# Two edits to the order of work: a weight split ahead of candidate steps, and a yield in the last attention

## The chip, the cores and the metric

The kernel runs on one core of a Trainium2 chip. The metric is the device time of one execution in microseconds, the median of several runs; shorter is better. A core has five engines with an instruction queue each: TensorE (PE in the profile) for matmuls, VectorE (DVE), ScalarE (ACT), GpSimd (POOL) and SyncE (SP), which issues most of the DMAs. Each queue is worked off in order; semaphores hold an instruction until its inputs are there.

## What is computed

One transformer layer on 1024 tokens of width 1024, batch 1, with float32 inputs. The parts that matter here:

```python
proj = h @ w_in[l]                       # q, k, v of 8 + 8 heads, forget logits
fox_out = forgetting_attention(...)      # causal softmax with a log-forget bias
sb_out = stick_breaking_attention(...)   # causal, in log space, a cumulative sum per row
x = x + gt1 * (mixed @ w_out[l])
h2 = rms_norm(x, g_norm_ffn[l]) * (1.0 + sc2) + sh2
x = x + gt2 * peer_layer(h2, w_query[l], sub_keys[l], expert_down[l], expert_up[l])
return rms_norm(x, g_final)

def peer_layer(h, w_query, sub_keys, expert_down, expert_up):
    query = (ht @ w_query).reshape(t, PEER_HEADS, 2, PEER_HALF)
    sub_scores = jnp.einsum('thpd,hpkd->thpk', query, sub_keys)
    half_vals, half_idx = lax.top_k(sub_scores, PEER_TOPK)           # 16 of 128, twice
    cand = half_vals[:, :, 0, :, None] + half_vals[:, :, 1, None, :]
    top_vals, top_pos = lax.top_k(cand.reshape(...), PEER_TOPK)      # 16 of the 16 x 16 sums
    ...                                                              # expert numbers, softmax gates
    act = gelu(jnp.einsum('td,thkd->thk', xb, expert_down[eb])) * gb
    return jnp.einsum('thk,thkd->td', act, expert_up[eb])
```

## The kernel before

The 1024 tokens are eight tiles of 128. Tiles 0 to 4 form block A, tiles 5 to 7 block B. Each block goes through norm, projection (`proj`), `attention`, output projection (`post`), second norm (`post_b`) and routing (`route`). Routing takes the 16 half-heads one after another: a panel of 24 matmuls with weights split into a high and a low part, the key scores, and the top 16 of 128 by VectorE's MAX, FIND_INDEX and MATCH_REPLACE (L886 to L890). From eight (head, tile) rows at a time `cands` (L930) forms the 50 candidate sums that can be among the top 16 (L946 to L951), searches them (L958 to L962), unpacks the positions (L966 to L978), picks the expert numbers bit by bit (L982 to L999) and makes the gates (L1004 to L1018). It is a generator: each `yield` ends a step. Up to L978 there are seven steps. Block A's candidates run inside its routing; block B's three generators are kept (`b.rest`, L924) for later.

In the front, streams of such generators are merged by `mrg` (L276): each stream has a weight and a count of credit that its yields have cost so far, and the stream with the least credit per weight is taken next. `mrg((rA, TOT_RB), (attention(bB, mixB, atp), TOT_B))` at L1149 merges the rest of block A's routing (weight 60) with block B's attention (weight 70). What the streams issue is then put into the engines' queues by a scheduler that has its own estimate of times, so that the order in a queue is not the order of the calls.

The feed-forward layer is done in two ways. For tiles 5 to 7 (`sparse`, L1208) the rows of the 128 experts of a token are gathered from HBM by GpSimd (L1221, L1234) and worked on by VectorE (L1223, L1239). For tiles 0 to 4 all 16384 experts are computed densely in 128 chunks of 128 experts; block A's gates lie in HBM as a dense table. A chunk's weights `wfd` and `wfu` are loaded by SP (L1270, L1272), split into high and low parts (`dh`, `uh` on ScalarE, L1289 and L1297; `dl`, `ul` on VectorE, L1292 and L1300), multiplied (`gelu_s`, L1302, two halves of 24 matmuls into the PSUM tile `sp`, GELU on ScalarE at L1308), multiplied by the gates (`mul_g`, L1310) and split again. After four chunks `up` (L1328) multiplies with the second weights. In this stage the order on TensorE, VectorE and ScalarE is that of the calls among themselves; instructions of the front may stand between them. Between the dense calls, `sp_(n)` issues n steps of block B's remaining candidates and then of the gathers: `sp_(PUMP_0)` with 7 steps at L1369, two steps in the first chunk, one and one in the later ones, five and two in the second half of a group.

Of the kernel before, what the change touches and what calls it, by code (L numbers as in the profile page):

```python
# [50 lines left out]
PUMP_0 = 7  # L51
# [54 lines left out]
def tile_kernel(ctx: ExitStack, tc: tile.TileContext, x, ccol, w_ada, badac, bgt2, gcols, w_in, w_f, bf_, gout,  # L106
# [473 lines left out]
    def attention(b, mixed, pool):  # L580
# [4 lines left out]
        def load_kq(pi):  # L585
            t = [pool.tile([P, b.ht], F32R, name=n_, tag=n_) for n_ in ("qa", "qb")]
            for n_, t_ in enumerate(t):
                dma(t_.bitcast(F32), qsp[pi, n_, :, qs_].bitcast(F32))
            t.append(pool.tile([P, b.ht], F32R, name="qla", tag="qla"))
            for h_ in (la, lb):  # L590
                dma(t[2][h_].bitcast(F32), qsp[pi, 2, la, qs_].bitcast(F32))
            k = [pool.tile([P, nk_], F32R, name=n_, tag=n_) for n_ in ("ka", "kb")]
            for n_, t_ in enumerate(k):
                dma(t_.bitcast(F32), ksp[pi, n_, :, 0:nk_].bitcast(F32))
            fb = pool.tile([P, nk_], F32, name="fb", tag="fb")
            dma(fb, fcd[pi:pi + 1, 0:nk_].to_broadcast([P, nk_]))
            L[pi] = t + k + [fb]
# [3 lines left out]
        def load_v(pi):  # L601
            vv = pool.tile([P, nk_], F32, name="vv", tag="vv")
            dma(vv, vsp[pi, :, 0:nk_])
            LV[pi] = vv
            LB[pi] = pool.tile([P, b.ht], F32R, name="qlb", tag="qlb", bufs=b.nq)
            for h_ in (la, lb):
                dma(LB[pi][h_].bitcast(F32), qsp[pi, 2, lb, qs_].bitcast(F32))
# [5 lines left out]
            yield -1  # L613
        load_kq(0)
        load_v(0)
        n = 8 * nt
        U = {}
        pair = {}
# [505 lines left out]
    atp = pool(st_at, "atA", 2)  # L1124
    mixA = xtile(xp, bA, "mixA")
    mrg((attention(bA, mixA, atp), 110), (ad2, max(1.0, 24 - AD1)), bg=((pp, PP2), (zr, ZR2)))
    st_at.close()
    rp = rpl[0] = pool(rps, "rp", side="right")
# [18 lines left out]
    mixB = xtile(xp, bB, "mixB")  # L1147
    soft_rs[0] = RS1
    mrg((rA, TOT_RB), (attention(bB, mixB, atp), TOT_B))  # L1149
    st_at.close()  # L1150
    am[0], ax[0] = ALS[2]()
# [94 lines left out]
    def pump(n):  # L1246
        while n > 0 and bgs:
            if next(bgs[0], 0) == 0:
                bgs.pop(0)
            else:  # L1250
                n -= 1
# [23 lines left out]
    def loadg(gi):  # L1275
        i1 = gi * CG
        dma = nc.sync.dma_start if gi > 1 else G.dma_start
        gg = dp.tile([P, CG, P], F32, name="gg", tag="gg", bufs=2)
        g2 = dp.tile([P, CG, P], F32, name="gg2", tag="gg2", bufs=1)
        for k in range(2):  # L1280
            dma((gg, g2)[k], gds[k].rearrange("(p c t) o -> p c (t o)", p=P, t=P)[:, i1:i1 + CG])
        g4 = dp.tile([P, NPT * P // SB, CG, SB], F32, name="g4", tag="g4", bufs=2)
        dma(g4, gd[:, :, i1 * SB:(i1 + CG) * SB].rearrange("s p (c t) -> p s c t", t=SB))
        return gg, g4, g2

    def split_d(k, act):
        if act:
            k.dh = dp3.tile([P, D], F32R, name="dh", tag="dh", bufs=2)
            S.activation(k.dh, k.wfd, AF.Copy)  # L1289
        else:  # L1290
            k.dl = dp3.tile([P, D], F32R, name="dl", tag="dl", bufs=2)
            V.tensor_sub(k.dl, k.wfd, k.dh.bitcast(F32))  # L1292
# [63 lines left out]
    def sp_(n):  # L1356
        pump(n)
# [4 lines left out]
    def nextload():  # L1362
        i1 = next(loads, None)
        if i1 is not None:
            ready.append(load(i1))

    for _ in range(WB):
        nextload()
    sp_(PUMP_0)  # L1369
    nxt = ready.pop(0)  # L1370
    split_d(nxt, True)
    split_d(nxt, False)
    gcur = loadg(0)
    for gi in range(NG):
        grp = []
# [100 lines left out]
```

## Time and profile before

| | |
|---|---|
| median of 3 runs | 3056.48 us (3053.08 to 3063.33) |
| profiled execution | 3071.45 us, its span 3069.7 us |
| TensorE matmuls busy | 2895.8 us (94%) |
| weight loads of TensorE | 2675.8 us (87%), beside the matmuls |
| VectorE busy | 2588.3 us (84%) |
| ScalarE, GpSimd busy | 1189.7 us (39%), 1365.3 us (44%) |
| moved by DMA | 856.93 MB, 279 GB/s on average |

The front lasts to about 1218 us of the span, the dense stage with the gathers beside it from there to the end. Shares of the whole span are averages over stages with different limits; the tables of stretches below separate them. A timeline row gives start, duration, engine, line, operation and tiles; in brackets stands how long the engine was idle before and what ended that.

### The profile page before, as it was taken

The page shows a single profiled execution, that of the slowest core. Times are in us where ns is not written, and L with a number is a line of the kernel's source. Part 1 is how long each engine was busy: PE and PEld are TensorE (multiplying, and loading weights), DVE is VectorE, ACT ScalarE, POOL GpSimd, SP SyncE. Part 2 cuts the span into 40 slices and gives each one's busy share as a digit, 9 for nine tenths or more (in the row PEclk, how much of TensorE's full clock was granted, in tenths as well). Part 3 has the DMA queues.
Part 4 walks back from the last instruction along what each step waited for, and adds up shares of the span by engine and source line. Part 5 has one row for each costly group of instructions (what it writes and reads, how often), then busy time and mean ns, then how long its engine had stood idle before and what let it go on. Part 6 is the DMA issues. An engine that isn't in the chain of part 4 may idle for free.

```text
span 3069.7 us, 48010 instructions
## 1 busy us (share of the span) xinstructions
PE 2895.8 (94%) x17472; PEld 2675.8 (87%) x17472; DVE 2588.3 (84%) x5282; ACT 1189.7 (39%) x2148; POOL 1365.3 (44%) x964
## 2 busy tenths in 40 slices
PE   5899998997989897889999999999999999999997
PEld 4899898997879897789898898998998989989986
DVE  6677554899997788889898998898989989989987
ACT  5566655445676763322132222231221222312212
POOL 0000000056756000055666665666666666666661
PEclk9999999998999998899999999999999999999998
DMA  7999454667435576379999999999999999999995
GB/s 256 285 346 280 142 198 177 211 183 197 105 82 165 217 266 241 104 277 354 350 354 339 334 355 338 344 361 347 343 344 332 346 345 342 364 332 343 340 328 196
DMA packets 368317, 856.93 MB, mean 279 GB/s; under 512 B 48952, under 2 KB 172880, under 8 KB 366032
## 3 DMA queue, kind: packets, MB, share of 16 engines
q1 hardware_dynamic: 236032, 440.08, 41.6%
q0 software_dynamic: 132048, 413.79, 38.3%
q8 instruction: 137, 2.24, 0.3%
q14 instruction: 100, 0.82, 0.1%
HBM read 742.49 MB, written 111.25 MB: 278 GB/s over the span
## 4 chain that ended last, share of the span: by engine, by line
PE 48%; DVE 22%; DMA 13%; issue 9%; ACT 4%; POOL 4%; SPq 0%; DVEq 0%; POOLq 0%; ACTq 0%
DMA ring<-in_eup,e 7%; PE sp L379 6%; PE sp L381 6%; PE sp L380 6%; DVE sacc L1239 4%; POOL ring L1234 3%; PE po L1333 3%; PE po L1335 3%; PE po L1334 3%; PE tp L1077 2%; PE av L706 2%; DMA wa<-in_w_ada 2%; PE proj L379 2%; PE pers L1333 2%; PE pers L1334 2%
## 5 line engine op out<-in xcount | busy, mean ns | idle before, releaser
L1234 POOL DMA_INDIRECT ring<-in_eup,e x384 | 557.5, 1452 | 289.7 <-DVE sacc L1239 150.3
L1221 POOL DMA_INDIRECT ring<-in_edown,e x384 | 519.2, 1352 | 373.3 <-DVE ring L1223 151.2
L379 PE MATMUL sp<-hT,dl 128*128 128x320 f32 x2048 | 636.5, 311 | 26.5 <-DVE dl L1292 16.1
L380 PE MATMUL sp<-hT,dh 128*128 128x320 f32 x2048 | 635.7, 310 | 0.0
L381 PE MATMUL sp<-hT,dh 128*128 128x320 f32 x2048 | 635.6, 310 | 0.0
L1239 DVE SCALAR_TENSOR_TENSOR sacc<-ring,sdot,sacc 128x1024 f32<-128x1024 f32 x381 | 488.2, 1281 | 66.8 <-DMA ring<-in_eup,e 62.2
L1223 DVE SCALAR_TENSOR_TENSOR ring<-ring,sx 128x1024 f32<-128x1024 f32 x384 | 460.7, 1219 | 67.2 <-DMA ring<-in_edown,e 66.1
L379 PEld LDWEIGHTS sp<-hT,dl 128*128 128x128 f32 x2048 | 387.1, 189 | 29.6 <-DVE dl L1292 15.3
L1297 ACT ACTIVATE uh<-wfu 128x1024 fp32r<-128x1024 f32 x128 | 134.8, 1053 | 680.3 <-PE po L1335 680.3
L380 PEld LDWEIGHTS sp<-hT,dh 128*128 128x128 f32 x2048 | 387.1, 189 | 1.2
L381 PEld LDWEIGHTS sp<-hT,dh 128*128 128x128 f32 x2048 | 387.0, 189 | 0.0
L1039 POOL DMA_INDIRECT gds<-g,e x128 | 238.5, 1863 | 263.0 <-DMA wf<-in_w_in 137.5
L1333 PE MATMUL po<-ul,ch 128*128 128x512 f32 x768 | 305.9, 398 | 21.1 <-DVE accB L1342 11.9
L1334 PE MATMUL po<-uh,ch 128*128 128x512 f32 x768 | 301.1, 392 | 0.0
L1335 PE MATMUL po<-uh,cl 128*128 128x512 f32 x768 | 301.1, 392 | 0.0
L1308 ACT ACTIVATE ge<-sp 128x320 f32<-128x320 f32 x256 | 110.4, 433 | 443.6 <-PE sp L381 443.5
L1333 PEld LDWEIGHTS po<-ul,ch 128*128 128x128 f32 x768 | 145.4, 189 | 66.0 <-DVE accB L1342 28.8
L1334 PE MATMUL pers<-uh,ch 128*128 128x512 f32 x512 | 199.6, 390 | 0.0
L1333 PE MATMUL pers<-ul,ch 128*128 128x512 f32 x512 | 199.5, 390 | 0.0
L1335 PE MATMUL pers<-uh,cl 128*128 128x512 f32 x512 | 199.2, 389 | 0.0
L303 POOL TENSOR_TENSOR i<-ms,mhalf 128x4 f32<-128x4 f32 (+1 forms) x16 | 22.4, 1400 | 338.7 <-DVE ms L301 338.7
L1335 PEld LDWEIGHTS po<-uh,cl 128*128 128x128 f32 x768 | 145.4, 189 | 31.2
(307 smaller groups left out, 6534.4 us busy)
## 6 DMA issues: line engine op xcount, KB each, us to landing
wfd<-in_wdense SPq DMA_DIRECT2D x128, 512.0 KB, 6.7
wfu<-in_wdense SPq DMA_DIRECT2D x128, 512.0 KB, 6.6
gd<-gt SPq DMA_DIRECT2D x16, 2048.0 KB, 8.3
g<-gd SPq DMA_DIRECT2D x30, 1024.0 KB, 14.9
wa<-in_w_ada SPq DMA_DIRECT2D x96, 256.0 KB, 5.3
wf<-in_w_in SPq DMA_DIRECT2D x48, 512.0 KB, 4.5
gds<-zt SPq DMA_DIRECT2D x32, 512.0 KB, 6.2
gg<-gds SPq DMA_DIRECT2D x60, 256.0 KB, 6.5
```

The costliest lines, as they stand in the source:

```text
L379: PE.matmul(pt, wl[:, c], hh[:, kd, cs], start=kd == 0, stop=False)
L380: PE.matmul(pt, wh[:, c], hl[:, kd, cs], start=False, stop=False)
L381: PE.matmul(pt, wh[:, c], hh[:, kd, cs], start=False, stop=kd == KD - 1)
L1039: G.indirect_dma_start(out=gds[nsct[0]], out_offset=off, in_=b.g[:, c_:c_ + 1], in_offset=None, compute_op=OP.add)
L1221: G.indirect_dma_start(out=r, out_offset=None, in_=edown, in_offset=bass.IndirectOffsetOnAxis(ap=bs.e[:, c_:c_ + 1], axis=0))
L1223: (V.scalar_tensor_tensor(r, r, 1.0, sx, op0=OP.mult, op1=OP.mult, accum_out=s_[:, j:j + 1]))
L1234: G.indirect_dma_start(out=r, out_offset=None, in_=eup, in_offset=bass.IndirectOffsetOnAxis(ap=bs.e[:, c_:c_ + 1], axis=0))
L1239: (V.scalar_tensor_tensor(acc, r, s_[:, j:j + 1], acc, op0=OP.mult, op1=OP.add))
L1297: S.activation(k.uh, k.wfu, AF.Copy)
L1333: PE.matmul(po, k.ch[:, tcs], k.ul[:, ds_], start=c == 0 and (gi == 0 or not per), stop=False)
L1334: PE.matmul(po, k.ch[:, tcs], k.uh[:, ds_], start=False, stop=False)
L1335: PE.matmul(po, k.cl[:, tcs], k.uh[:, ds_], start=False, stop=c == CG - 1 and (gi == NG - 1 or not per))
```

## The change

First, `sp_(PUMP_0)` moves behind the two calls that split the first chunk's `wfd`. Second, `attention` yields once with a credit of 10 after the loads of its first head pair are issued, for block B alone (`b.t0` is 0 for block A).

```diff
--- before.py
+++ after.py
@@ -613,6 +613,8 @@
             yield -1
         load_kq(0)
         load_v(0)
+        if b.t0:
+            yield 10.0
         n = 8 * nt
         U = {}
         pair = {}
@@ -1366,10 +1368,10 @@
 
     for _ in range(WB):
         nextload()
-    sp_(PUMP_0)
     nxt = ready.pop(0)
     split_d(nxt, True)
     split_d(nxt, False)
+    sp_(PUMP_0)
     gcur = loadg(0)
     for gi in range(NG):
         grp = []
```

On VectorE, at the start of the dense stage before the change (L886 to L890 are top-k work of block B's routing, L976 to L978 the end of the seven candidate steps, `dl` the low part of a chunk's first weights):

```order
L976 TENSOR_TENSOR af<-af,tm 128x128
L977 SCALAR_TENSOR_TENSOR bq<-tm,bq 128x128
L888 MATCH_REPLACE sr<-v_12766,scs 128x128
L889 MAX v_12766<-sr 128x8
L978 SCALAR_TENSOR_TENSOR bq<-pos,bq 128x128
L889 MAX v_12766<-sr 128x8
L890 MAX_INDEX i_12767<-v_12766,sr 128x8 x2
L888 MATCH_REPLACE sr<-v_12766,scs 128x128
L889 MAX v_12766<-sr 128x8
L890 MAX_INDEX i_12767<-v_12766,sr 128x8
L1292 TENSOR_TENSOR dl<-wfd,dh 128x1024 x2
L1300 TENSOR_TENSOR ul<-wfu,uh 128x1024
```

The candidate steps stand among the top-k work, and the first two `dl` follow each other.

The same place after the change (line numbers are higher by two):

```order
L890 MATCH_REPLACE sr<-v_12766,scs 128x128 x2
L891 MAX v_12766<-sr 128x8 x2
L892 MAX_INDEX i_12767<-v_12766,sr 128x8 x2
L1294 TENSOR_TENSOR dl<-wfd,dh 128x1024
L938 CAST ifl<-i_12767 128x256
L948 TENSOR_TENSOR cand<-v_12766 128x8x16
L948 TENSOR_TENSOR cand<-v_12766 128x8x8
L948 TENSOR_TENSOR cand<-v_12766 128x8x5
L948 TENSOR_TENSOR cand<-v_12766 128x8x4
```

No candidate step stands ahead of the first `dl` any more; the cast that opens them and the sums follow it.

The place where they end, after the change:

```order
L978 TENSOR_TENSOR af<-af,tm 128x128
L979 SCALAR_TENSOR_TENSOR bq<-tm,bq 128x128
L980 SCALAR_TENSOR_TENSOR bq<-pos,bq 128x128
L1294 TENSOR_TENSOR dl<-wfd,dh 128x1024
L1302 TENSOR_TENSOR ul<-wfu,uh 128x1024
L984 CAST bi<-af 128x128
L988 TENSOR_SCALAR bt<-bi 128x128
```

The second `dl` and the first `ul` now come behind the last of the seven steps.

On TensorE, the first scores of block B's attention before the change (`proj<-hT` is a panel of block A's routing, `sc<-ka` and `sc<-kb` the scores of the two heads of a pair):

```order
L379 MATMUL proj<-hT,wl 128x256
L380 MATMUL proj<-hT,wh 128x256
L381 MATMUL proj<-hT,wh 128x256
L641 MATMUL sc<-ka,qla 128x512
L644 MATMUL sc<-ka,qa 128x512
L641 MATMUL sc<-ka,qla 128x256
L643 MATMUL sc<-mfox,identr 128x128
L644 MATMUL sc<-ka,qa 128x256
L641 MATMUL sc<-kb,qlb 128x512
L644 MATMUL sc<-kb,qb 128x512
L641 MATMUL sc<-kb,qlb 128x256
```

The scores of both heads follow each other, behind the last panel.

The same place after the change:

```order
L379 MATMUL proj<-hT,wl 128x256
L380 MATMUL proj<-hT,wh 128x256
L381 MATMUL proj<-hT,wh 128x256
L643 MATMUL sc<-ka,qla 128x512
L646 MATMUL sc<-ka,qa 128x512
L643 MATMUL sc<-ka,qla 128x256
L645 MATMUL sc<-mfox,identr 128x128
L646 MATMUL sc<-ka,qa 128x256
L879 MATMUL proj<-kt,qf 128x128 x2
L379 MATMUL proj<-hT,wl 128x256
L380 MATMUL proj<-hT,wh 128x256
L381 MATMUL proj<-hT,wh 128x256
```

Another panel with its key scores (L879) stands between the first head's scores and the second's; one of 24 matmuls with 384 columns was also moved ahead of the first scores.

## Rows read from the trace of the kernel before

**Rows 1.** Table of stretches: length, busy us by engine, clock, DMA.

```profile
690.00:940.00 250.00, 218.56 (x1490) 201.88 (x1490) 234.85 (x830) 163.72 (x341) 165.25 (x91) 0.89 0.49 118
...
940.00:1200.00 260.00, 245.32 (x1767) 236.95 (x1766) 220.03 (x616) 179.04 (x303) 34.90 (x18) 0.99 0.65 238
...
1240.00:3060.00 1820.00, 1784.90 (x9918) 1616.59 (x9916) 1623.64 (x2296) 459.52 (x669) 1090.14 (x791) 0.99 0.91 328
```

**Rows 2.** Waits of TensorE from 1230 us on: total, times, longest.

```profile
PE po L1333 <- DVE accB L1342: 11.9, 11, 5.3
PE sp L379 <- ACT ge L1308: 9.5, 2, 7.7
```

**Rows 3.** Timeline of VectorE, dense start: start, us, operation, [idle before].

```profile
1226.15 1.23 DVE L1292 TENSOR_TENSOR dl<-wfd,dh 128x1024 fp32r<-128x1024 f32 x1 [8.39 <-ACT dh L1289]
1228.71 1.23 DVE L1292 TENSOR_TENSOR dl<-wfd,dh 128x1024 fp32r<-128x1024 f32 x1 [1.33 <-ACT dh L1289]
1229.85 1.22 DVE L1300 TENSOR_TENSOR ul<-wfu,uh 128x1024 fp32r<-128x1024 f32 x1
...
1240.20 0.68 DVE L1314 TENSOR_TENSOR gg<-gg,gg 128x512 f32<-128x512 f32 x1
```

**Rows 4.** Timeline of VectorE, a later group's candidate steps with nothing between.

```profile
1289.42 0.28 DVE L936 CAST ifl<-i 128x256 bf16<-128x256 uint32 x1
...
1300.86 0.29 DVE L976 TENSOR_TENSOR af<-af,tm 128x128 f32<-128x128 f32 x1
...
1301.39 0.23 DVE L975 TENSOR_SCALAR tm<-pos 128x128 f32<-128x128 f32 x1
...
1306.34 1.22 DVE L1292 TENSOR_TENSOR dl<-wfd,dh 128x1024 fp32r<-128x1024 f32 x1
```

**Rows 5.** Timeline of VectorE, the same two operations among top-k work.

```profile
1206.94 0.26 DVE L976 TENSOR_TENSOR af<-af,tm 128x128 f32<-128x128 f32 x1
1207.13 0.28 DVE L977 SCALAR_TENSOR_TENSOR bq<-tm,bq 128x128 f32<-128x128 f32 x1
1207.33 0.28 DVE L889 MAX8 v<-sr 128x8 f32<-128x128 f32 x1
```

**Rows 6.** Timeline of TensorE, three starts after an idle stretch.

```profile
1227.43 0.64 PE L379 MATMUL sp<-hT,dl 128*128 128x320 f32 x1 [15.16 <-DVE dl L1292]
...
1246.08 0.41 PE L379 MATMUL sp<-hT,dl 128*128 128x320 f32 x1 [1.75 <-ACT ge L1308]
...
1322.71 0.63 PE L379 MATMUL sp<-hT,dl 128*128 128x320 f32 x1 [7.74 <-ACT ge L1308]
```

**Rows 7.** Timeline of ScalarE, GELU of the first two chunks.

```profile
1237.33 0.44 ACT L1308 ACTIVATE ge<-sp 128x320 f32<-128x320 f32 x1 [1.74 <-PE sp L381]
...
1245.59 0.77 ACT L1308 ACTIVATE ge<-sp 128x320 f32<-128x320 f32 x2
```

**Rows 8.** Chain of waits, last slow matmul of the second and the last start.

```profile
1250.14 0.23 PE sp L380
...
1328.68 0.21 PE sp L379
```

**Rows 9.** Timeline of VectorE, last routing scores of block B.

```profile
1212.88 0.68 DVE L886 MAX8 v<-scs 128x8 f32<-128x128 f32 x3 [0.80 <-ACT scs L879]
...
1217.48 0.28 DVE L890 FIND_INDEX8 i<-v,sr 128x8 uint32<-128x128 f32 x1
```

**Rows 10.** Timeline of TensorE, last routing panel.

```profile
1202.82 0.69 PE L379 MATMUL sc<-hT,wl 128*128 128x384 f32 x1 [1.64 <-DMA wl<-wsp]
```

**Rows 11.** Timeline of TensorE, first scores of the last attention.

```profile
707.24 0.56 PE L641 MATMUL sc<-ka,qla 128*128 128x512 f32 x1 [2.05 <-DMA ka<-ksp]
...
712.54 0.76 PE L641 MATMUL sc<-kb,qlb 128*128 128x512 f32 x1 [3.67 <-DMA qla<-qsp]
```

**Rows 12.** Table of stretches, start and end of the last attention.

```profile
700.00:715.00 15.00, 8.74 (x47) 7.45 (x46) 12.83 (x58) 2.57 (x11) 7.21 (x5) 0.73 1.06 343
...
930.00:940.00 10.00, 10.00 (x68) 10.00 (x68) 1.69 (x7) 4.59 (x9) 7.97 (x6) 0.69 0.21 2
```

## The prediction

> **What bounds the kernel now.** I read four views in this order: the table of stretches, the waits of TensorE, the timelines of VectorE, TensorE and ScalarE around the two edits, and the chain of waits there.
>
> The table of stretches [rows 1] shows three regimes. During the last attention (690 to 940 us) VectorE is busy 234.85 of 250 us and TensorE 218.56: VectorE sets the pace. From 940 to 1200 us (one-hot products and block B's routing) TensorE has 245.32 of 260 us and VectorE 220.03. In the dense stage TensorE has 1784.90 of 1820 us. So a delay at the start of the dense stage has little to be absorbed in: the two largest waits of TensorE from 1230 us on are 11.9 us for evacuations, spread over the whole stage, and 9.5 us for GELU, both of whose pieces (1.75 and 7.74 us) lie in its first 100 us [rows 2, 6].
>
> At the start of the dense stage the reader is to see a queue on one engine. VectorE waits 8.39 us for the first chunk's weights, then makes dl of chunk 0, dl of chunk 1 and ul of chunk 0, then does two candidate steps, and comes to the gates of chunk 0 at 1240.20 us [rows 3]. Behind those gates ScalarE has a candidate's exponential, and behind that the GELU of chunk 1 at 1245.59 us; only that frees the PSUM tile with which TensorE starts chunk 2 at 1246.08 us [rows 6, 7]. VectorE's queue, not the matmuls, decides when chunk 2 starts.
>
> **The change part by part.** First edit, the seven candidate steps. They are the first cast, the candidate sums, eight small top-k searches and the unpacking up to L978. Nothing is added or removed, only the place differs. Before, the order has them mixed into the top-k work of block B's routing, where VectorE had them done before it sat idle for the weights. In the changed order the first dl stands ahead of all of them, and dl waits for the load; so the 8.39 us in which VectorE waits stay empty, and the steps run afterwards, between dl of chunk 0 and dl of chunk 1. POOL's and SP's instructions are not moved by this edit: the seven steps issue no DMA. Their two ScalarE copies go behind the first dh and ahead of the second, which has time.
>
> What the steps cost there is seen at a later group, which ran them alone: from the cast at 1289.42 to the dl that follows at 1306.34, 16.92 us [rows 4]. The new times: dl of chunk 0 at 1226.15, plus 1.14 (start to start of such a pair, 1228.71 to 1229.85 [rows 3]) gives 1227.29; plus 16.92 gives 1244.21; dl of chunk 1 takes 1.14 more, so ul of chunk 0 starts at 1245.35 instead of 1229.85. That is 15.5 us late, and so is all that is queued behind it: the two further steps, the gates (1255.7), the GELU (1261.1), and chunk 2 on TensorE (1261.6). TensorE does chunk 0 as before, until 1237.33 [rows 7], stands for 8 us until the second dl is there, takes about 9.9 us for chunk 1 (1227.43 to 1237.33 for chunk 0, which also came after an idle stretch [rows 6, 7]), and stands again for about 6 us where it stood for 1.75.
>
> After a wait TensorE runs for a while at the lower of its two clock levels, 1.2 instead of 2.4 GHz. After 7.74 us of idle the slow matmuls last from 1322.71 to 1328.68, 6.0 us; after 1.75 us they end 4.1 us behind the start [rows 6, 8]. A wait of 6 us instead of 1.75 therefore costs up to half the difference, 0.9 us. Together 16.4 us at chunk 2, and from there to the end I find no slack.
>
> What the move gives back in front: the last scores come to VectorE at 1212.88 and its last index is found at 1217.48 plus 0.28 us [rows 9]; three of the moved operations stand between them in the order shown, at 0.2 us start to start [rows 5], 0.6 us. VectorE was waiting for these scores (0.80 us idle [rows 9]), so it had caught up, and the rest of the moved work hid behind TensorE. Bounds: TensorE's wait of 1.64 us for a late weight half [rows 10] and a slow stretch behind it, 4.1 us long as in [rows 8] and so worth 2.05, may vanish as the order of the last panels is another, 3.7 us saved; or one more such load is late, 1.6 us lost. I take 0.6 saved, since only that follows from the order.
>
> At this place a rule of the Trainium skill speaks for a lower price. The row first: two operations of the unpacking take 0.53 us from start to the next start when nothing stands between them, 1300.86 to 1301.39 [rows 4], and 0.39 us, 1206.94 to 1207.33, among top-k work [rows 5]. The Trainium skill (VectorE: DVE Perf Modes, section "The DRAIN you can't avoid") says that a semaphore between chained VectorE operations costs nothing extra. Read so, the steps would take no longer alone than in front. The trace does not agree for these short operations, and I keep the 16.92 us.
>
> Second edit, the yield in block B's attention. The order puts one more routing panel of 24 matmuls (384 columns) and another of 24 (256 columns) around the first scores. They cover the two waits of TensorE for the loads, 2.05 and 3.67 us [rows 11]. But VectorE paces this stage, and in that stretch it was idle for 15 minus 12.83, 2.2 us [rows 12]. The loads themselves are issued where they were. I take 2 us saved, nearest to that row. Bounds: all 5.7 us saved, if TensorE counted; or, as attention now stands later against routing, its end runs alone for longer: at 930 to 940 VectorE has 1.69 us of work [rows 12], and one more such stretch costs 8.3 us.
>
> Sum: 16.4 - 0.6 - 2.0 = 13.8 us more. The profiled execution took 3071.45 us with a span of 3069.7; it would take 3085.2. That execution is 15 us above the median of the runs shown, 3056.48, and I put the same 13.8 us on the median: 3070.3 us.
>
> **The rivals.** First, the dense stage covers most of it. TensorE needs only dl of chunk 1 in time; its stall is 1245.35 minus 1237.33, 8.0 us, and what comes later is caught up. With the same gains: 8.0 - 2.6 = 5.4, 3061.9 us. For it: TensorE holds a chunk of work ahead. Against it: chunk 2 waited for the GELU already before [rows 6], and VectorE then has a long run of candidate steps.
>
> Second, on the other side: the front is paced by VectorE. In front the steps took about 16.92 x 0.39 / 0.53 = 12.4 us of its time. If VectorE was the late one at the end of routing, the dense stage starts 12.4 us earlier: 16.4 - 12.4 - 2.0 = 2.0, 3058.5 us, not slower by what can be told. It decides if VectorE comes late to the last scores; the 0.80 us for which it waited there [rows 9] and TensorE's larger share from 940 to 1200 [rows 1] speak against it.
>
> Third, the steps keep their price of the front, 12.4 us, when they stand alone: 16.4 - 4.5 - 2.6 = 9.3, 3065.8 us. This is the way in which the rule of the Trainium skill on the DRAIN would have it; [rows 4, 5] are against.
>
> Fourth, attention's end pays: 13.8 + 2.0 + 8.3 = 24.1, 3080.6 us. For it: the stream that starts later tends to end alone. Against it: in the order, the last scans of both kernels stand within one row of each other.
>
> **How the numbers follow.** I give the forecast 0.57, the first rival 0.13, the second 0.15, the third 0.05, the fourth 0.10. A measurement of this kernel tells a change from none at about 0.3%, 9.2 us, so slower begins at 3065.7. The forecast's own range, from the bounds of the front (3.7 saved to 1.6 lost) and of the attention (5.7 saved to a few lost), is 3063 to 3077; nine tenths of it are slower, 0.51. Half of the third and all of the fourth bring it to 0.63. Faster by over 9.2 us needs the second rival with all of the attention's gain and more, 0.05. The rest, 0.32, is no change. The range that holds 8 in 10 reaches to the second rival below and nearly to the fourth above: 3058 to 3079.
>
> **What would show it.** In the changed profile, the idle time of VectorE ahead of the first dl should still be 7 to 9 us; the cast should follow it and the second dl come 17 to 18 us behind the first; TensorE should stand about 8 us between chunks 0 and 1, and the GELU of chunk 1 should end some 35 us behind the first dl instead of 20. In the attention, the waits of 2.05 and 3.67 us should be gone while the stage's end moves by 2 us or less. I am wrong if chunk 2 starts less than 30 us behind the first dl, if the first dl itself moves by more than 6 us against the end of routing's first panels, or if TensorE's later waits shrink by what the start lost.

## The result and the profile after

The changed kernel takes 3094.73 us (median of 4 runs, 3083.85 to 3098.61); the kernel before took 3059.90 us beside it (4 runs, 3053.08 to 3064.88). The two medians lie 34.8 us apart. The ratio estimated from all these runs is 1.0093, with a 95% interval of 1.0070 to 1.0116: 21 to 36 us slower. Slower was forecast, but by 13.8 us; the time lies above the range of 3058 to 3079 us. The profiled execution took 3095.95 us with a span of 3094.2 us, 24.5 us more than that of before.

First the table of stretches of the changed kernel, with the columns of [rows 1].

```profile
690.00:940.00 250.00, 223.79 (x1429) 205.20 (x1427) 225.49 (x786) 157.50 (x325) 145.33 (x84) 0.85 0.49 118
...
1240.00:3060.00 1820.00, 1775.83 (x9914) 1614.72 (x9913) 1629.73 (x2365) 460.43 (x669) 1088.65 (x788) 0.99 0.91 326
```

In the last attention VectorE has 225.49 us of work instead of 234.85: the engine that paces the stage is idle more. In the same 1820 us of the dense stage TensorE works 9 us less.

Waits of TensorE from 1230 us on, as in [rows 2]:

```profile
PE sp L379 <- DVE dl L1294: 24.3, 5, 14.3
PE po L1335 <- DVE accB L1344: 15.2, 12, 5.3
PE sp L379 <- ACT ge L1310: 15.0, 2, 7.8
```

The waits for GELU have grown from 9.5 to 15.0 us, and those for dl have a new one of 8.94 us, which the timeline shows. TensorE's starts after an idle stretch, as in [rows 6] and [rows 10]:

```profile
1207.77 0.69 PE L379 MATMUL sc<-hT,wl 128*128 128x384 f32 x1 [3.88 <-DMA wl<-wsp]
...
1236.23 0.64 PE L379 MATMUL sp<-hT,dl 128*128 128x320 f32 x1 [14.26 <-DVE dl L1294]
...
1254.46 0.61 PE L379 MATMUL sp<-hT,dl 128*128 128x320 f32 x1 [8.94 <-DVE dl L1294]
...
1270.39 0.63 PE L379 MATMUL sp<-hT,dl 128*128 128x320 f32 x1 [7.18 <-ACT ge L1310]
...
1347.54 0.63 PE L379 MATMUL sp<-hT,dl 128*128 128x320 f32 x1 [7.77 <-ACT ge L1310]
```

VectorE at the same place, as in [rows 3]:

```profile
1234.95 1.23 DVE L1294 TENSOR_TENSOR dl<-wfd,dh 128x1024 fp32r<-128x1024 f32 x1 [7.21 <-ACT dh L1291]
1236.10 0.29 DVE L938 CAST ifl<-i 128x256 bf16<-128x256 uint32 x1
...
1253.09 1.23 DVE L1294 TENSOR_TENSOR dl<-wfd,dh 128x1024 fp32r<-128x1024 f32 x1
1254.23 1.22 DVE L1302 TENSOR_TENSOR ul<-wfu,uh 128x1024 fp32r<-128x1024 f32 x1
...
1264.51 0.69 DVE L1316 TENSOR_TENSOR gg<-gg,gg 128x512 f32<-128x512 f32 x1
```

The seven steps run alone from 1236.10 to 1253.09, 16.99 us, while 7.21 us of idle time stay empty ahead of them. The chain of waits shows how that reaches TensorE (start, us, what):

```profile
1254.23 1.22 DVE ul L1302
...
1264.51 0.70 DVE gg L1316
...
1267.25 0.29 DVE g L1006
1267.53 0.75 DVE cl L1328
1268.28 0.31 ACT g L1007
...
1268.61 1.28 ACT L1310
1269.90 0.45 ACT ge L1310
...
1270.39 0.63 PE sp L379
```

After ul come two further candidate steps and the gates, then a candidate's exponential on ScalarE (L1007), a load of ScalarE's function table (1.28 us), and only then the GELU that frees the PSUM tile of chunk 2.

The other place is the end of the last attention. Before, on VectorE (scan, last operation of block A's candidates, last mixB):

```profile
925.30 2.27 DVE L650 TENSOR_TENSOR_SCAN prs<-prs,zf 128x1024 f32<-128x1024 f32 x1
...
929.28 0.27 DVE L1020 TENSOR_SCALAR e<-tm,pidx 128x128 int32<-128x128 f32 x1
...
941.21 0.36 DVE L740 TENSOR_TENSOR mixB<-av,rs 128x192 f32<-128x192 f32 x1 [6.97 <-ACT mixB L738]
```

And after:

```profile
922.96 0.45 DVE L1022 TENSOR_SCALAR e<-tm,pidx 128x128 int32<-128x128 f32 x1
923.15 2.02 DVE L652 TENSOR_TENSOR_SCAN prs<-prs,zf 128x896 f32<-128x896 f32 x1
...
928.48 0.36 DVE L742 TENSOR_TENSOR mixB<-av,rs 128x192 f32<-128x192 f32 x1 [1.67 <-ACT mixB L740]
929.42 2.29 DVE L652 TENSOR_TENSOR_SCAN prs<-prs,zf 128x1024 f32<-128x1024 f32 x1 [0.59 <-ACT prs L689]
...
948.74 0.36 DVE L742 TENSOR_TENSOR mixB<-av,rs 128x192 f32<-128x192 f32 x1 [11.15 <-ACT mixB L740]
```

The last candidate operation stood behind the last scan; now it stands ahead of the last two, and nothing is left there to fill VectorE's waits of 1.67 and 0.59 us. The last mixB comes 7.5 us later.

Even that understates it: the instructions up to the last mixA of block A's attention are the same in all kernels here, yet the executions reach it at times between 405.9 and 419.2 us. So I count by stages, each from the mark of the column before to its own. The marks are starts in the timelines: the last `mixA<-av,rs` on VectorE, the last scan and the last `mixB<-av,rs` of block B's attention, the first dl, and TensorE's first matmul of chunk 2. All is in us; the last column is the ratio of the runs to those of before. A row is one profiled execution, the ratio many runs, so the two need not agree to a few us.

| kernel | to last mixA | to last scan | to last mixB | to first dl | to chunk 2 | to the end | ratio (95%) |
|---|---|---|---|---|---|---|---|
| before | 419.2 | 506.1 | 15.9 | 284.9 | 19.9 | 1823.6 | |
| after | 411.9 | 517.5 | 19.3 | 286.2 | 35.4 | 1823.8 | 1.0093 (1.0070 to 1.0116) |
| e1 yield alone | 417.6 | 515.0 | 19.3 | 284.1 | 19.9 | 1825.6 | 1.0026 (1.0010 to 1.0042) |
| e2 steps alone | 415.2 | 508.2 | 15.8 | 285.9 | 35.5 | 1826.2 | 1.0075 (1.0051 to 1.0099) |
| e3 yield of 5 | 414.5 | 501.2 | 21.5 | 282.8 | 19.9 | 1825.6 | 1.0020 (1.0006 to 1.0034) |
| e4 routing yields 20 | 405.9 | 501.5 | 14.3 | 288.2 | 19.9 | 1821.6 | 1.0013 (0.9999 to 1.0027) |
| e5 three steps behind | 414.2 | 505.5 | 12.9 | 282.8 | 29.5 | 1824.9 | 1.0036 (1.0021 to 1.0052) |
| e6 behind second dl | 414.7 | 508.6 | 13.9 | 286.0 | 36.8 | 1829.3 | 1.0078 (1.0049 to 1.0106) |
| e7 yield, weight 80 | 419.1 | 505.1 | 20.9 | 279.3 | 19.9 | 1822.3 | 1.0013 (0.9998 to 1.0028) |
| e8 weight 80 alone | 412.1 | 514.1 | 14.0 | 282.2 | 19.9 | 1822.2 | 1.0025 (1.0011 to 1.0040) |
| e9 nine steps in front | 410.6 | 507.2 | 15.9 | 284.8 | 18.1 | 1825.7 | 0.9984 (0.9965 to 1.0003) |
| e10 e9 and e4's yield | 409.2 | 502.4 | 17.2 | 288.4 | 18.2 | 1819.3 | 1.0003 (0.9988 to 1.0019) |
| e11 smaller blocks | 410.5 | 506.1 | 19.2 | 286.2 | 18.1 | 1835.7 | 1.0008 (0.9991 to 1.0025) |
| e12 smaller blocks, spread | 407.0 | 505.7 | 19.2 | 286.1 | 18.1 | 1843.9 | 1.0080 (1.0058 to 1.0102) |

After against before: -7.4, +11.5, +3.4, +1.3, +15.5, +0.2, together the 24.5 us of the two spans. Without the first stage, where nothing was changed, it is 31.9 us, inside the 21 to 36 of the ratio.

### The profile page after: what moved, and what is told of

Same layout as the page of the kernel before. It is cut to its first block, busy times and chain, and to the rows that moved or that the text cites. A ratio compares the mean times of both kernels' runs of the same rounds, so it can differ in the third digit from the quotient of the medians.

```text
span 3094.2 us, 48018 instructions
## 1 busy us (share of the span) xinstructions
PE 2905.0 (94%) x17472; PEld 2686.6 (87%) x17472; DVE 2590.0 (84%) x5282; ACT 1189.1 (38%) x2148; POOL 1355.8 (44%) x964
## 3 DMA queue, kind: packets, MB, share of 16 engines
q8 instruction: 137, 2.24, 0.3%
## 4 chain that ended last, share of the span: by engine, by line
PE 50%; DVE 21%; DMA 13%; issue 8%; ACT 4%; POOL 4%; SPq 0%; DVEq 0%; POOLq 0%; ACTq 0%
DMA ring<-in_eup,e 6%; PE sp L379 6%; PE sp L380 6%; PE sp L381 6%; DVE sacc L1241 3%; PE po L1335 3%; PE po L1336 3%; PE po L1337 3%; POOL ring L1236 3%; PE av L708 2%; PE tp L1079 2%; PE proj L379 2%; PE proj L380 2%; PE proj L381 2%; PE pers L1335 2%
## 5 line engine op out<-in xcount | busy, mean ns | idle before, releaser
L1041 POOL DMA_INDIRECT gds<-g,e x128 | 228.9, 1788 | 287.6 <-DMA wf<-in_w_in 138.1
L708 PEld LDWEIGHTS av<-vv,pt 128*128 128x128 f32 x1152 | 165.1, 214 | 15.8 <-ACT pt L722 7.5
L708 PE MATMUL av<-vv,pt 128*128 128x64 f32 x1152 | 165.9, 291 | 8.0 <-ACT pt L722 4.8
```

Source lines behind the costliest of these rows:

```text
L708: m_ = PE.matmul(av_[:, a, i, :], pt[:, q * P:(q + 1) * P], vv[:, kb_ * P + a * 64:kb_ * P + a * 64 + 64], start=kb_ == 0, stop=kb_ == qt)
L1041: G.indirect_dma_start(out=gds[nsct[0]], out_offset=off, in_=b.g[:, c_:c_ + 1], in_offset=None, compute_op=OP.add)
```

## The experiments

**One edit at a time (e1, e2).** e1 has only the second edit:

```diff
         load_v(0)
+        if b.t0:
+            yield 10.0
```

> The second edit alone: block B's attention yields once with a credit of 10; the seven steps stay ahead of the first split. Theory (the attention's end pays): VectorE sets the pace of this stage, and its work is the same; what decides is how far from the end of that work the last scan of the attention stands, because a serial tail of scan, exponential, transposes and matmuls follows it with VectorE idle. In the new order the last two scans stand behind the last candidate operation of block A instead of ahead of it. The last mixB should come at about 948.7 us (941.21 before) and the whole be 7 to 9 us longer than before. Rival 1 (the sum of the prediction): 2 us shorter, the later attention only covers waits for loads. Rival 2 (the two edits only cost this together): within 2 us of before.

Measured: 1.0026, that is 3 to 13 us; from the last mixA to the last mixB 534.4 us against 522.0. The last mixB came at 951.94. Rivals 1 and 2 fall. From the last mixA to the end the trace has 13.6 us more than that of before, a little above the interval; the profiled execution, 3083.33 us, is one of the two slowest of twelve (median 3072.72).

e2 has only the first edit:

```diff
-    sp_(PUMP_0)
     nxt = ready.pop(0)
     split_d(nxt, True)
     split_d(nxt, False)
+    sp_(PUMP_0)
```

> The first edit alone: the seven candidate steps stand behind the split of the first chunk, the attention is as before. Theory: the seven steps take 17 us on VectorE between the first and the second dl, chunk 2 starts 35 us behind the first dl instead of 20, and nothing later gives that back: 15 to 16 us longer than before, the last mixB unmoved at 941 us. Rival 1 (the dense stage covers most): 5 us longer. Rival 2 (the front was paced by VectorE and gives 12 us back): 2 to 4 us longer, with the first dl some 12 us earlier.

Measured: chunk 2 starts 35.46 us behind the first dl, the last mixB is not later (939.29), and the first dl stands 285.9 us behind it (284.9 before): the front gave nothing back. The ratio is 16 to 30 us; the trace's 15.5 us at the dense start and 2.6 behind it lie at the low end of that. Both ratios together give 1.0101, the change itself 1.0093: within the intervals the edits add.

**How much, and by which way (e5, e6).** e5 leaves four steps in front:

```diff
-    sp_(PUMP_0)
     nxt = ready.pop(0)
+    sp_(4)
     split_d(nxt, True)
     split_d(nxt, False)
+    sp_(3)
```

> Half a dose of the first edit: four of the seven candidate steps stay ahead of the first split, three (the last four small searches and the unpacking) stand behind it; the attention is as in the kernel before. Theory (every microsecond of steps between the first and the second dl delays chunk 2): in the changed kernel these three steps took from 1241.99 to 1253.09 us, 11.1 us, of the 17; so the second dl comes 12.2 us behind the first and chunk 2 starts 35.4 - 5.9 = 29.5 us behind it (19.9 before, 35.4 in the changed kernel). Rival (the first step behind dl does the harm, the rest is covered): 22 us or less, or still 35 us.

TensorE's starts in e5 (the first dl is at 1215.37):

```profile
1216.65 0.63 PE L379 MATMUL sp<-hT,dl 128*128 128x320 f32 x1 [14.36 <-DVE dl L1292]
...
1228.93 0.39 PE L379 MATMUL sp<-hT,dl 128*128 128x320 f32 x1 [3.56 <-DVE dl L1292]
...
1244.85 0.64 PE L379 MATMUL sp<-hT,dl 128*128 128x320 f32 x1 [7.12 <-ACT ge L1308]
```

Chunk 2 starts 29.48 us behind the first dl, as expected. The second dl comes 12.19 us behind the first, 9.63 us later than before, and chunk 2 is 9.55 us late: the dose passes through in full. e6 moves all seven behind the second dl:

```diff
             if c < CG - 1 and not hasattr(nxt, "dl"):
                 split_d(nxt, False)
+            if gi == 0 and c == 0:
+                sp_(PUMP_0)
```

> The seven steps stand behind the second dl instead of between the first and the second; the attention is as in the kernel before. TensorE then has the weights of chunk 1 in time. Theory (chunk 2 waits for the queue on VectorE: ul and the gates of chunk 0, and ScalarE's work behind them): the stall of 8.94 us between chunks 0 and 1 goes, but chunk 2 still starts 35 to 37 us behind the first dl, and the time is that of the first edit alone, 15 to 17 us longer than before. Rival (it is the late second dl that costs): chunk 2 starts 26 to 28 us behind the first dl, and half of the loss is gone.

TensorE's starts in e6 (first dl at 1223.16):

```profile
1224.44 0.63 PE L379 MATMUL sp<-hT,dl 128*128 128x320 f32 x1 [14.18 <-DVE dl L1292]
...
1260.00 0.64 PE L379 MATMUL sp<-hT,dl 128*128 128x320 f32 x1 [19.16 <-ACT ge L1308]
```

The wait for the second dl is gone and chunk 2 still starts 36.84 us behind the first dl. So the wait between chunks 0 and 1, the most striking new row of the profile, costs nothing by itself; the queue of ul, steps and gates does.

**What the yield does (e3, e4, e7, e8).** e3 has `yield 5.0` in place of 10.

> As the second edit alone, but with a credit of 5 instead of 10. In the order on VectorE this puts the last scan of the attention 20 rows nearer to the start than before (and 19 nearer than with a credit of 10), with candidate work of block A behind it; in the kernel before, the 20 rows up to the last scan took 10.1 us (915.20 to 925.30). Theory (the place of the last scan on VectorE decides, not the yield): the last mixB comes at 931 to 935 us instead of 941.21, and the whole is 5 to 9 us shorter than before. Rival 1 (attention started later ends later, in proportion to the credit): 3 to 5 us longer than before. Rival 2 (the prediction's: only the waits for the first loads change): 1 to 2 us shorter.

The last scan came early, as its place in the order says (501.2 us behind the last mixA), but what follows took 21.5 us, and the last mixB was no earlier (522.7). The expected gain did not come; the ratio is even 1.0020, which the stages of its one trace do not explain. In e4 the other stream yields:

```diff
-    mrg((rA, TOT_RB), (attention(bB, mixB, atp), TOT_B))
+    def head():
+        yield 20.0
+    mrg((chain(head(), rA), TOT_RB), (attention(bB, mixB, atp), TOT_B))
```

> The opposite of the second edit: the rest of block A's routing yields once with a credit of 20 at the start of the merge, so that the attention is ahead of it. In the order on VectorE the last scan stands 35 rows nearer to the start than before, and the last candidate operation behind the last mixB. Theory (the place of the last scan decides): the last mixB comes at 925 to 933 us, the tail runs beside candidate work, and the whole is 6 to 12 us shorter than before. Rival 1 (VectorE's total work in the stage decides, whichever stream ends last): within 3 us of before. Rival 2 (an attention that starts earlier waits longer for its first loads, 5.7 us of TensorE's waits before): 2 to 6 us longer.

The last mixB came at 921.66 us, but 13 of those 19.5 us were there at the last mixA already. By stages the attention is 6.2 us shorter and the way from there to the first dl 3.3 us longer, and the ratio shows no gain. The expected 6 to 12 us shorter did not come.

e7 and e8 take the late start and the order at the end apart. e7 is e1 with `TOT_B = 80.0` instead of 70; e8 is the kernel before with that weight alone.

> The second edit alone (credit 10), and the weight of block B's attention in the merge is 80 instead of 70, so that the attention, started late, catches up: in the order on VectorE the last candidate operation of block A stands again behind the last scan, as before; with the yield alone it stood ahead of the last two scans. Measured from the last mixA to the last mixB (522.0 us before, 534.4 with the yield alone). Theory A (the end decides: routing's work runs out first and the last scans and their tail find VectorE idle): 521 to 527 us, and at most 3 us longer than before. Theory B (the late start decides: VectorE gets its work 10 us later and never makes it up): 531 to 537 us.

> No edit of the change; only the weight of block B's attention in the merge is 80 instead of 70. In the order on VectorE the last candidate operation of block A stands ahead of the last two scans, as with the yield of 10, although the attention starts as early as before. From the last mixA to the last mixB (522.0 us before, 534.4 with the yield alone): Theory A (the end decides): 530 to 537 us, 7 to 12 us longer than before. Theory B (the late start decides): 519 to 525 us, no longer than before.

The table of stretches, one row for each kernel, from 285 us behind the last mixA to the last scan. Before:

```profile
704.24:925.30 221.06, 196.02 (x1357) 179.54 (x1356) 214.93 (x728) 152.93 (x310) 144.85 (x78) 0.92 0.49 122
```

After:

```profile
696.87:929.42 232.55, 206.34 (x1330) 187.75 (x1328) 213.04 (x726) 152.77 (x315) 132.83 (x76) 0.86 0.49 118
```

e7, late start, the end as before:

```profile
704.05:924.15 220.10, 195.04 (x1333) 178.52 (x1333) 211.20 (x720) 152.29 (x310) 119.99 (x70) 0.91 0.50 125
```

e8, early start, the end as after:

```profile
697.13:926.25 229.12, 202.38 (x1341) 183.70 (x1339) 216.86 (x730) 152.46 (x314) 148.93 (x81) 0.89 0.48 118
```

VectorE's work is nearly the same in all four, 211 to 217 us. What differs is its idle time: 6.1 us before, 19.5 after, 8.9 in e7, 12.3 in e8 (16.7 in e1). By the mark that the expectations name, the last mixB, e7 came at 526.0 us, inside Theory A's range, and e8 at 528.1, between the two ranges. Up to the last scan the length goes with the order at the end, not with the late start. Over all kernels that have the end of before, the last scan stands 505.1 to 508.6 us behind the last mixA (before, e2, e5, e6, e7, e9, e11, e12); with the candidates ahead of the last two scans it is 514.1 to 517.5 (after, e1, e8).

But only a part of the idle time lies at the end. VectorE's waits for scores in the same stretch, before:

```profile
DVE prf L667 <- PE sc L644: 1.6, 1, 1.6
...
DVE t L672 <- PE sc L644: 1.0, 3, 0.6
```

After:

```profile
DVE t L674 <- PE sc L646: 7.9, 6, 3.3
DVE prf L669 <- PE sc L646: 4.8, 4, 1.5
```

Together they are 2.6 us before and 12.7 after (9.7 in e1, 6.5 in e8, 5.8 in e7): most of the new idle time is spent waiting for TensorE's scores. The first 20 and the last 50 us of the stretch, before:

```profile
704.24:724.24 20.00, 12.60 (x61) 10.48 (x60) 18.13 (x54) 8.21 (x25) 9.90 (x6) 0.74 0.87 276
875.30:925.30 50.00, 44.97 (x334) 40.28 (x335) 49.61 (x131) 40.17 (x85) 39.71 (x22) 0.97 0.28 37
```

After:

```profile
696.87:716.87 20.00, 16.45 (x103) 15.02 (x101) 14.76 (x65) 8.54 (x22) 7.74 (x5) 0.83 1.04 326
879.42:929.42 50.00, 44.73 (x305) 41.23 (x303) 44.38 (x101) 35.96 (x76) 39.45 (x23) 0.87 0.26 21
```

In the last 50 us VectorE is idle for 0.4 us before and 5.6 after (8.6 in e1, 5.8 in e8, 3.7 in e7), in the first 20 us for 1.9 before and 5.2 after (2.9 in e1). Between the last candidate operation and the last scan it is idle for 2.3 us after and in e1, and for 4.5 in e8. So the end has some 5 of the changed kernel's 13.4 us; the rest is spread over the stage, and why the scores come late there is not shown.

A rival is TensorE's clock: the mean granted clock of the four stretches is 0.92, 0.86, 0.91 and 0.89, and in the changed kernel TensorE is busy for 10.3 us longer with fewer matmuls. It cannot be all of it: e2 and e6, with the order of before, had 0.90 in this stretch and took 223.2 and 223.6 us; e1 and e8 had 0.89 and took 230.1 and 229.1.

The ratios agree less sharply: e7, at 1.0013, can be told neither from no loss nor from the yield's, and e8, with the early start, is at 1.0025. And on to the first dl, e8 is 810.3 us behind the last mixA, within the 801.1 to 811.5 us of the kernels whose attention is as before (806.9 in before itself), while e1 is at 818.5 and the changed kernel at 823.1. That the yield costs time is shown; that the order at its end is the cause is shown only in part.

The stretch from the last scan to the last mixB is another matter. After:

```profile
929.42:948.74 19.32, 18.92 (x117) 18.78 (x115) 5.58 (x11) 7.48 (x17) 15.14 (x10) 0.65 0.20 1
```

e8, the same 117 matmuls:

```profile
926.25:940.28 14.03, 13.16 (x117) 12.37 (x115) 5.58 (x11) 7.47 (x17) 9.80 (x7) 1.00 0.18 1
```

With TensorE at a mean granted clock of 0.65 it lasts 19.32 us, at 1.00 14.03 us. The kernels with the order of before at this place show 12.9 us at 0.88 (e5) to 19.2 (e11, e12 below). So of the yield's cost the 9 us up to the last scan in e1 (11.5 in the changed kernel) lie outside what the same order does by itself; the 3.4 us behind it do not, and stay open.

**Attempts at a faster kernel (e9 to e12).** e9 sets `PUMP_0 = 9`, so that two more steps fall into VectorE's idle wait.

> The opposite of the first edit: nine candidate steps instead of seven stand ahead of the first split, the rest as in the kernel before. The two more steps took 9.2 us on VectorE between ul and the gates of chunk 0 (1230.98 to 1240.20 in the kernel before), and VectorE is idle for 8.39 us ahead of the first dl. Theory (VectorE's queue between the first dl and the gates sets chunk 2; work put into the idle wait is free): the idle wait shrinks to 1 us or less, the first dl moves by 1 us at most, the gates of chunk 0 come some 4 to 6 us behind the first dl instead of 14, and chunk 2 starts 17.5 to 19 us behind it instead of 19.9, as then only the matmuls of chunk 1 hold it up. With the later steps spread over more chunks the waits of 7.7 us at 1288 and 1323 us may go too: 2 to 12 us shorter in all. Rival (the front is held up by two more steps): the first dl comes 5 us or more later against the last mixB, and nothing is gained.

VectorE in e9:

```profile
1218.55 1.22 DVE L1292 TENSOR_TENSOR dl<-wfd,dh 128x1024 fp32r<-128x1024 f32 x1
1220.39 1.23 DVE L1292 TENSOR_TENSOR dl<-wfd,dh 128x1024 fp32r<-128x1024 f32 x1 [0.62 <-ACT dh L1289]
```

The idle time is gone, the first dl is no later (284.8 us behind the last mixB), and the last GELU of chunk 1 runs at 1236.88, 18.3 us behind the first dl, with no wait of TensorE for chunk 2. But the waits come back further on. Waits of TensorE in e9 from 1215 us on:

```profile
PE sp L379 <- ACT ge L1308: 12.7, 2, 11.8
...
PE po L1333 <- ACT accB L1340: 5.2, 1, 5.2
```

ScalarE stands behind a candidate's exponential, whose input is late (timeline of ScalarE in e9):

```profile
1253.55 1.28 ACT L1005 ACT_TABLE_LOAD   x1
1271.58 0.31 ACT L1005 ACTIVATE g<-g 128x128 f32<-128x128 f32 x1 [16.74 <-DVE g L1004]
```

From the first dl to the end it is 1843.9 us, 1843.6 before. The median is 3056.52 us against 3063.01, the ratio 0.9984 (0.9965 to 1.0003): a gain is not shown. e10 is e9 with e4's yield.

> Nine steps ahead of the first split, and the rest of block A's routing yields 20 at the start of the last attention, so that the attention is ahead. The attention's stage as with that yield alone (515.8 us from the last mixA to the last mixB, against 522.0 before), the dense start as with nine steps alone. If both gains add: 5 to 15 us shorter than before. If the output projection and routing behind the attention are longer by what the attention's stage saves (288.2 us from the last mixB to the first dl with that yield alone, 284.9 before): no better than nine steps alone.

1.0003 (0.9988 to 1.0019), with 519.6 us for the attention and 288.4 us from there to the first dl: no better than nine steps alone. e11 deals the steps out in smaller blocks:

```diff
-                sp_(PUMP_C - (prev is not None))
+                sp_(PUMP_C - (gi == 1) - (prev is not None))
-        sp_(PUMP_U)
+        sp_(2 if gi == 0 else PUMP_U + (2 <= gi < 13))
-            sp_(PUMP_V)
+            sp_(1 if gi == 0 else PUMP_V)
```

> Nine steps ahead of the first split, and the steps of the first two groups are dealt out in smaller blocks: in the first group two steps instead of five behind the fourth chunk and one instead of two behind each evacuation, in the second one per chunk instead of two; eleven later groups take one step more, so that the sum by the end is about the same. With nine steps alone TensorE's start was 2 us better, but further on it waited 5.2 us for an evacuation and 11.8 us for GELU (7.7 and 7.7 before), because ScalarE stood 16.74 and 15.17 us behind a candidate's exponential whose input came late from VectorE. Theory (it is blocks of steps on VectorE that hold up ScalarE and then TensorE): both waits fall below 3 us, the dense stage from the first dl to the end takes 1828 to 1836 us instead of 1843.6, and the time is 7 to 15 us below that of before. Rival (what is taken out of the first groups comes back as waits in the second, or at the end behind the gathers): within 5 us of nine steps alone.

Waits of TensorE in e11 from 1210 us on:

```profile
PE po L1333 <- DVE accB L1342: 32.1, 22, 5.3
PE sp L379 <- DVE dl L1292: 17.1, 6, 15.1
...
```

The long waits at the start are gone, and more than that is lost at the evacuations of the later groups, where the eleven steps went: 1853.8 us from the first dl to the end, ratio 1.0008 (0.9991 to 1.0025). In e12 those eleven stand in the groups' first chunks, `sp_(... + (c == 0 and 2 <= gi < 13))`.

> As the smaller blocks, but the one step more of eleven later groups stands in the group's first chunk instead of ahead of the evacuations. With it ahead of the evacuations the start of the dense stage had lost its long waits, but TensorE waited 32.1 us for evacuations (22 times), 11.9 us (11 times) before: what the start gained was given back there. Theory (a step is free in a chunk, whose matmuls take 10 us against 5 us of VectorE's work, and not ahead of an evacuation): the waits for evacuations fall back to about 12 us, the long ones at the start stay away, the dense stage from the first dl to the end takes 1828 to 1836 us (1843.6 before), and the time is 7 to 15 us below that of before. Rival (gathers set the pace: starting them a group later lengthens the end by as much): dense stage 1842 us or more, no faster than before.

Waits of TensorE in e12 from 1210 us on:

```profile
PE sp L379 <- DVE dl L1292: 38.6, 12, 15.1
PE po L1333 <- DVE accB L1342: 19.5, 11, 5.3
```

1.0080 (1.0058 to 1.0102), 1862.1 us from the first dl to the end: the step in the first chunk makes the next dl late, eleven times. Against the kernel before, TensorE's waits are 22.5 us longer for dl, 7.6 longer for the evacuations by VectorE and 9.5 shorter for GELU. A chunk did not have the room that I took it to have.

## Why the prediction was wrong

**The first edit was right, and so was its way.** Dl of chunk 1 was to come 17 to 18 us behind the first; it came 18.14 behind. VectorE's idle time ahead of the first dl, 7 to 9 us: 7.21. TensorE's wait between chunks 0 and 1, about 8 us: 8.94. GELU of chunk 1 was to end some 35 us behind the first dl; it starts 34.95 us behind it and ends 35.72. Chunk 2 was to be 15.5 us late and lose 0.9 more at the lower clock; it is 15.5 us late, and from there to the end 0.2 more are lost. e5 and e6 show that VectorE's queue is the way. The first rival (the dense stage covers it) falls with that, and the third too: alone the steps took 16.99 us, not the 12.4 estimated for the front. The Trainium skill (VectorE: DVE Perf Modes, section "The DRAIN you can't avoid") says that a semaphore between chained VectorE operations costs nothing extra. Read as the prediction read it, the steps would have kept the price of the front; the trace does not bear that reading out for these short operations.

**The front gave nothing back.** Of 0.6 us forecast nothing is seen: the first dl stands 286.2 us behind the last mixB, 284.9 before, and 285.9 in e2. TensorE's wait for the late weight half grew from 1.64 us [rows 10] to 3.88 us, by 2.24; the bound allowed 1.6. The second rival, 12.4 us back, falls.

**The step that failed is the second edit's: "I take 2 us saved, nearest to that row."** The measured sign is the other one: 14.9 us longer from the last mixA to the last mixB in the changed kernel, 12.4 in e1. I looked at the start of the stage, where the loads are waited for [rows 11, 12], and took VectorE's 2.2 us of idle time there as what could be saved. TensorE's waits for the loads shrank, to 0.44 and 2.92 us, but VectorE's idle time did not: in the first 20 us of the stretch above it grew from 1.9 to 5.2 us (2.9 in e1). Up to the last scan VectorE is idle for 13.4 us more, 10.1 of them waits for TensorE's scores, to which the prediction gave no term. The fourth rival named the end ("its end runs alone for longer"), but its price was 8.3 us and its chance 0.10, because "the last scans of both kernels stand within one row of each other". They do (two instructions of VectorE apart); but the row number tells how much VectorE has done before a scan, not what is left to fill its waits. That stood in the same order: the last candidate operation had moved from behind the last scan to ahead of the last two. This goes with some 5 of the 13.4 us; for the rest the cause stays open.

With 14.9 in place of -2.0 and 1.3 in place of -0.6 the sum is 32.6 us; the stages give 31.9.

**The base was short as well.** I put the sum on a median of 3 runs, 3056.48 us. Later medians of the same kernel were 3059.9 to 3064.8. And the two profiled executions differ by 7.4 us before the first changed instruction, so that the 24.5 us between their spans are less than what the change cost in them.

## What to carry to other kernels

When two streams are merged and one ends in a serial chain, look at which stream's last work stands behind the other's last scan, not only at how far down the row is: filler that ends before the chain leaves its last waits empty. And price a stage by what its pacing engine waits for, all along the stage: here that engine did the same work in 11.5 us more. Work on an in-order queue is free only in a wait that is there already; moved behind the instruction that waits, 16.99 us of it cost 15.5 us here, through whatever stands behind it on the next engine. Last, split two spans by marks that both traces have, before comparing them: what was not changed may differ by as much as what was.

## What the runs showed of the hardware

Not expected: the time to one and the same mark, with the same instructions ahead of it, differs by 13.4 us between the profiled executions of the fourteen kernels (405.9 to 419.2 us). The stretch with the same 117 matmuls at the attention's end lasts 14.03 us at a mean granted clock of 1.00 and 19.32 at 0.65. And a candidate's exponential between two GELUs on ScalarE costs two loads of its function table, 1.28 us each: in the changed kernel one at 1266.98, ahead of the exponential at 1268.28, and one at 1268.61 behind it, which stands on the chain above.
